# Matmul with layer norm: row quarters loaded for two row tiles at a time, and moved behind the last pieces of B

## The chip, the core and the metric

One Trainium2 chip; the kernel uses one of its cores. Times are device microseconds of one execution. The trace comes from one profiled execution, and its times count from the start of that span.

## The reference

```python
m, k, n = 2048, 2048, 2048        # a: m x k, b: k x n, float32
x = np.matmul(a, b)
mean = np.mean(x, axis=-1, keepdims=True)
var = np.var(x, axis=-1, keepdims=True)
normalized = (x - mean) / np.sqrt(var + eps)
return (gamma * normalized + beta).astype(np.float32)
```

## The kernel before

**Tiling.** The 2048 rows of `a` are sixteen row tiles of 128 (index `i`, or `g` for the first four). The inner dimension is sixteen pieces of 128 (index `t` or `kt`), and the 2048 columns are four banks of 512 (index `q`). One matmul multiplies a 128x128 piece of the transposed row tile (`at[i]`) by a 128x512 piece of B in float16 (`b16`) and adds it up in a PSUM bank (`mm`, L149). There are eight PSUM banks. Before row tile 15, 64 matmuls make one row tile.

**Loading B.** B arrives as 32 float32 pieces of 128x1024 (512 KB): sixteen left halves (`w_0_…`) and sixteen right halves (`w_1_…`). `load_b` (L77) puts each into a slot of the pool `bigp`. `cast_left` and `cast_right` turn it into float16, VectorE (DVE) one half of the columns (L82, L87), ScalarE (ACT) the other (L83, L88). A slot can be filled again when both casts are done. Later in the kernel the same pool holds the output tiles.

**Loading A.** The first three quarters (512 columns) of row tiles 0 to 3 arrive as `load_first`, 256 KB each (L99), are cast (L104), transposed on PE against `ident` (L110) and copied out of PSUM (L114). The twelve of them are numbered `n`; number 7 is the second quarter of row tile 3. All other quarters come through `load_part` (L123): four DMAs of 64 KB, one for each group of 32 partitions, in runs of 512 bytes. ACT casts such a quarter into a buffer of `a16p` (`cast_part`, L133), and DVE transposes it in 32x32 blocks into `at[i]` (`transpose_part`, L140). The pool `firstp` has four slots of 4 KB per partition, each for two row pieces or two quarters. Row tiles 6 to 15 are loaded from POOL's queue, everything before from SP's.

**Stages.** The order of instructions on each engine is the order in the program. (1) Pieces 0 to 3 are multiplied for row tiles 0 to 3, left half first, then right half; the sums are put by in SBUF (`put_by`, L162 and L164). (2) Pieces 0 to 3 for row tile 4, which needs its first quarter. (3) Pieces 4 to 15, left half, for row tiles 0 to 3; the sums put by are added (`add_up`, L168). (4) The same for the right half: pieces 4 to 13 over eight banks, then for each of the eight banks pieces 14 and 15 and an `add_up` on DVE; after them eight `stats` (bn_stats, L157) of these sums. (5) Row tile 4, pieces 4 to 15, bank by bank: bank 0 runs over its twelve pieces before bank 1 starts. Pieces 4 to 7 need the row tile's second quarter, 8 to 11 the third, 12 to 15 the last. (6) Row tiles 5 to 14, bank by bank, sixteen pieces each, while DVE takes statistics, transposes quarters of the row tile two ahead, and normalises (L173 to L191). (7) Row tile 15 in six spans of columns, and its tail.

**The order of loads on SP** is written out by hand in L321 to L354: B's pieces 0 to 3 with the first row pieces; row tile 4's first quarter; B's left pieces 4 to 15 with row pieces and, after pieces 8 to 11, the last quarters of row tiles 0 to 3; B's right pieces 4 to 13; row tile 4's other three quarters (`p_1_207`, `p_2_212`); B's right pieces 14 and 15 (`w_1_221`, `w_1_223`); row tile 5 (`p_0_225`, `p_2_234`); gamma and beta.

Names in the trace: `ps_q_…` are PSUM banks, `x_q_…` sums in SBUF, `bnst` statistics, `at_425` to `at_428` the transposed row tiles 0 to 3, `at_638` row tile 4, `at_1015` row tile 5.

Of the kernel before, what the change touches and what calls it, by code (L numbers as in the profile page):

```python
# [9 lines left out]
FP32 = mybir.dt.float32  # L10
# [5 lines left out]
def kernel(  # L16
# [19 lines left out]
    nc = tc.nc  # L36
    P = 128
    M, K = a.shape
    _, N = b.shape
    n_mt = M // P  # L40
    n_kt = K // P
# [4 lines left out]

    konst = ctx.enter_context(tc.tile_pool(name="konst", bufs=1))
    bpool = ctx.enter_context(tc.tile_pool(name="bpool", bufs=1))
    bigp = ctx.enter_context(tc.tile_pool(name="bigp", bufs=7))
    firstp = ctx.enter_context(tc.tile_pool(name="firstp", bufs=4))  # L50
    first16 = ctx.enter_context(tc.tile_pool(name="first16", bufs=2))
    a16p = ctx.enter_context(tc.tile_pool(name="a16p", bufs=8))
    atp = ctx.enter_context(tc.tile_pool(name="atp", bufs=6))
    xpool = ctx.enter_context(tc.tile_pool(name="xpool", bufs=20))
    upool = ctx.enter_context(tc.tile_pool(name="upool", bufs=2))
# [14 lines left out]
    a_pieces = a.rearrange("(s r) (c q k) -> q c r s k", r=32, c=4, q=4)  # L70

    bnst, x_of, mv_of, rs_of, at = {}, {}, {}, {}, {}
    a_in, b_in, t_of, tile_in, part = {}, {}, {}, {}, {}

    def load_b(kt, h, queue=None):
        w = bigp.tile([P, NH], FP32, tag="big", name=f"w{kt}_{h}")
        (queue or nc.sync).dma_start(w, b_rows[kt // 4, kt % 4][:, ds(h * NH, NH)])  # L77
        b_in[kt, h] = w

    def cast_left(kt):  # L80
        w = b_in.pop((kt, 0))
        nc.vector.tensor_copy(b16[:, kt, 0:NB], w[:, 0:NB])  # L82
        nc.scalar.copy(b16[:, kt, NB:NH], w[:, NB:NH])  # L83

    def cast_right(kt):
        w = b_in.pop((kt, 1))
        nc.vector.tensor_copy(b16[:, kt, NH:NH + NB], w[:, 0:NB])  # L87
        nc.scalar.copy(b16[:, kt, NH + NB:N], w[:, NB:NH])  # L88
# [3 lines left out]
    def load_first(n):  # L92
        g, c = pieces[n]
        if n % 2 == 0:
            a_in[n + 1] = firstp.tile([P, 2, 4 * P], FP32, tag="first", name=f"f{g}_{c}")
            a_in[n] = a_in[n + 1][:, 0]
        else:
            a_in[n] = a_in[n][:, 1]
        nc.sync.dma_start(a_in[n], a[ts(g, P), ts(c, 4 * P)])  # L99

    def cast_first(n):
        h = first16.tile([P, P, 4], FP16, tag="h", name=f"h{n}")
        copy = nc.scalar.copy if n in (2, 3) else nc.vector.tensor_copy
        copy(h.rearrange("m p t -> m (p t)"), a_in[n])  # L104
        a_in[n] = h

    def turn_first(n):
        t_of[n] = psum.tile([P, 4, P], FP16, tag="c_ps", bufs=8, name=f"t_ps{n}")
        for t in range(4):
            nc.tensor.transpose(t_of[n][:, t, :], a_in[n][:, :, t], ident)  # L110

    def keep_first(n):
        g, c = pieces[n]
        nc.vector.tensor_copy(at[g][:, ds(4 * c, 4), :], t_of[n])  # L114

    def new_parts(parts):
        f = firstp.tile([P, 2, 4, P], FP32, tag="first", name="p%d_%d" % parts[0])
        for j, x in enumerate(parts):
            tile_in[x] = f[:, j]

    def load_part(i, c, queue=None):
        for q in range(4):
            (queue or nc.sync).dma_start(  # L123
                tile_in[i, c][ds(32 * q, 32)], a_pieces[q, c][:, ds(4 * i, 4)])

    def load_half(i, h, queue=None):
        new_parts([(i, 2 * h), (i, 2 * h + 1)])
        load_part(i, 2 * h, queue)
        load_part(i, 2 * h + 1, queue)

    def cast_part(i, c):
        a16 = a16p.tile([P, 4, P], FP16, tag="a16", name=f"a{i}_{c}")
        nc.scalar.copy(a16, tile_in[i, c])  # L133
        tile_in[i, c] = a16

    def new_at(i):
        at[i] = atp.tile([P, n_kt, P], FP16, tag="at", name=f"at{i}")

    def transpose_part(i, c):
        nc.vector.transpose(  # L140
            at[i][:, ds(4 * c, 4), :].rearrange("p t (s r) -> p s t r", r=32),
            tile_in[i, c].rearrange("p s (k t) -> p s t k", t=4),
        )

    def bank(i, q):
        x_of[i, q] = psum.tile([P, NB], FP32, tag="c_ps", bufs=8, name=f"ps_{i}_{q}")

    def mm(i, q, kt, lo=0, hi=n_kt):
        nc.tensor.matmul(  # L149
            x_of[i, q], at[i][:, kt, :], b16[:, kt, ds(q * NB, NB)],  # L150
            start=(kt == lo), stop=(kt == hi - 1),
        )

    def stats(i, q):
        if i not in bnst:
            bnst[i] = stat.tile([P, n_nb, 6], FP32, tag="bnst", name=f"bnst{i}")
        nc.vector.bn_stats(bnst[i][:, q, :], x_of[i, q])  # L157

    def put_by(i, q):
        part[i, q] = xpool.tile([P, NB], FP32, tag="x_sb", name=f"x_{i}_{q}")  # L160
        if q % 2:
            nc.vector.tensor_copy(part[i, q], x_of[i, q])  # L162
        else:
            nc.scalar.copy(part[i, q], x_of[i, q])  # L164

    def add_up(i, q):
        x = part[i, q]
        nc.vector.tensor_tensor(x, x_of[i, q], x, AluOp.add)  # L168
        x_of[i, q] = x
# [136 lines left out]
    with tc.manual_schedule(engines=order):  # L306
# [13 lines left out]
        K1 = 4  # L320
# [7 lines left out]
        for t in range(K1):  # L328
            load_b(t, 1)
            if t:  # L330
                load_first(K1 + t - 1)
        load_first(2 * K1 - 1)
        new_parts([(4, 0)])
        load_part(4, 0)
        for t in range(K1, n_kt):
            load_b(t, 0)
            if K1 + t < len(pieces):
                load_first(K1 + t)
            elif t < n_kt - K1:
                g = t % K1  # L340
                if g % 2 == 0:
                    new_parts([(g, 3), (g + 1, 3)])
                load_part(g, 3)
        for t in range(K1, n_kt - 2):
            load_b(t, 1)
        new_parts([(4, 1)])
        load_part(4, 1)
        load_half(4, 1)
        for t in range(n_kt - 2, n_kt):
            load_b(t, 1)  # L350
        for h in (0, 1):
            load_half(5, h)
        nc.sync.dma_start(gamma_b, gamma.unsqueeze(0).to_broadcast([P, N]))
        nc.sync.dma_start(beta_b, beta.unsqueeze(0).to_broadcast([P, N]))  # L354
        for i in range(6, n_mt):
# [66 lines left out]
            if t < 2:  # L422
                turn_first(K1 + t)
        bank(*late)
        cast_first(2 * K1 - 1)
        waits = list(range(K1))
        for j, (g, q) in enumerate(early):
            mm(g, q, K1 - 1, 0, K1)
            put_by(g, q)
            if j in (4, 6):  # L430
                n = K1 + j // 2
                turn_first(n)
                keep_first(n)
            if j in (1, 3, 5):
                mm(*late, waits.pop(0), 0, K1)
        for t in waits:
            mm(*late, t, 0, K1)
        cast_part(4, 0)
        new_at(4)
        transpose_part(4, 0)  # L440
        put_by(*late)


        for q in range(n_nb):
            bank(4, q)
        cast_left(K1)
        cast_first(2 * K1)
        for q in range(n_nb):
            for t in range(K1):
                mm(4, q, t, 0, K1)  # L450
            put_by(4, q)


# [3 lines left out]
        for t in range(K1, n_kt - 3):  # L457
            n = K1 + t
            if K1 < t <= 2 * K1:
                keep_first(n - 1)  # L460
            if K1 < t < 2 * K1:
                cast_first(n)
            cast_left(t + 1)
            if 2 * K1 <= t < 3 * K1:
                cast_part(t % K1, 3)
                transpose_part(t % K1, 3)
            if t == 2 * K1:
                bank(*late)
                for u in range(K1, t):
                    mm(*late, u, K1)  # L470
            for g, q in early[:5]:
                mm(g, q, t, K1)
            if t < 2 * K1:
                turn_first(n)
            for g, q in early[5:]:
                mm(g, q, t, K1)
            if t >= 2 * K1:
                mm(*late, t, K1)
# [10 lines left out]
        for g, q in right:  # L489
            bank(g, q)  # L490
        for t in range(K1 + 3, n_kt):
            if t == n_kt - 2:
                for c in (1, 2):
                    cast_part(4, c)
                    transpose_part(4, c)
            cast_right(t)
            if t - K1 - 3 < len(left):
                stats(*left[t - K1 - 3])
        for t in range(K1, n_kt - 2):
            for g, q in right:  # L500
                mm(g, q, t, K1)
        cast_part(4, 3)
        for j, (g, q) in enumerate(right):
            for t in (n_kt - 2, n_kt - 1):
                mm(g, q, t, K1)
            add_up(g, q)
            if j == 1:
                transpose_part(4, 3)
        for g, q in right:
            stats(g, q)  # L510
        new_at(5)
        for c in range(4):
            cast_part(5, c)
            transpose_part(5, c)

# [64 lines left out]
```

## Time and profile before

| What | Value |
|---|---|
| median of 3 runs | 248.38 us (248.35 to 249.16) |
| profiled execution, its own time | 248.16 us |
| its span in the trace | 246.3 us |
| PE busy | 231.7 us, 94% |
| DVE busy | 201.3 us, 82% |
| ACT busy, POOL busy | 96.9 us, 89.3 us |
| DMA, mean over the span | 214 GB/s |
| mean granted PE clock | 0.989 |

The span runs from the first to the last instruction on the core; the execution's own time has 1.86 us around it. A busy share is an average over stages that have different limits, so the waits and the chain of work that ended last say more than it does. In the chain each step is followed back to what released it. A DMA's "us to landing" counts from its issue to its completion. The issue itself takes the queue some 0.3 to 0.4 us, and a queue that waits before an issue shows a gap between issues.

### The profile page before, as it was taken

Reading aid. Unit: us, or ns where it says so; the run is one execution under the profiler, and the core shown is the slowest. Engines: PE = TensorE matmul, PEld = TensorE weight load, DVE = VectorE, ACT = ScalarE, POOL = GpSimd, SP = SyncE. Lnnn points to the kernel's source line nnn. Section 1 sums busy time; section 2 is a strip of 40 time slices with the busy share of each in tenths; the row PEclk is TensorE's granted clock in tenths of the full one; section 3 lists DMA queues with packets and bytes.
Section 4 is the critical chain, followed back from the end, with each engine's and each line's share of the span. In section 5 each row is a group of like instructions: output and inputs, shape, how many; then the busy total and the mean of one; then the engine's idle time right before and its main releaser. Section 6 shows DMA issues by size and latency. Waiting matters only on the chain.

```text
span 246.3 us, 3405 instructions
## 1 busy us (share of the span) xinstructions
PE 231.7 (94%) x1121; PEld 107.3 (44%) x1121; DVE 201.3 (82%) x373; ACT 96.9 (39%) x197; POOL 89.3 (36%) x168
## 2 busy tenths in 40 slices
PE   8999799799989999999999999999999999999960
PEld 2444344344434444444444444444444444446440
DVE  1468664498349999999999999999999997866962
ACT  3474523544323604027190918263553673020020
POOL 0000000000539369977666680779284000000011
PEclk9999999999999999999999999999999999999995
DMA  6999999999598955857466664657375413030404
GB/s 197 380 404 309 390 248 277 391 412 339 124 293 196 319 150 189 283 186 253 134 200 203 222 212 182 185 200 254 134 257 174 170 48 122 14 159 0 170 3 170
DMA packets 23857, 52.66 MB, mean 214 GB/s; under 512 B 4640, under 2 KB 11296, under 8 KB 23584
## 3 DMA queue, kind: packets, MB, share of 16 engines
q1 hardware_dynamic: 18432, 41.74, 48.5%
q0 software_dynamic: 5120, 10.50, 16.2%
q10 hardware_dynamic: 288, 0.21, 0.3%
q8 instruction: 9, 0.15, 0.2%
q14 instruction: 8, 0.07, 0.1%
HBM read 35.65 MB, written 16.78 MB: 213 GB/s over the span
## 4 chain that ended last, share of the span: by engine, by line
PE 74%; DMA 16%; DVE 5%; SPq 1%; issue 1%; DVEq 0%; ACT 0%; ACTq 0%
DMA w_1_205<-in_b_dram 4%; DMA w_0_160<-in_b_dram 3%; DMA w_0_185<-in_b_dram 3%; DMA f_2_148<-in_a_dram 3%; DMA w_1_223<-in_b_dram 3%; PE w_ps L314 2%; DMA w_0_173<-in_b_dram 2%; PE ps_1_2256 L149 1%; PE ps_1_2129 L149 1%; PE ps_2_2039 L149 1%; PE ps_3_1941 L149 1%; PE ps_0_1874 L149 1%; PE ps_1_1771 L149 1%; PE ps_2_1673 L149 1%; PE ps_3_1569 L149 1%; PE ps_0_1502 L149 1%
## 5 line engine op out<-in xcount | busy, mean ns | idle before, releaser
L223 ACT ACTIVATE junk<-b_93 128x1024 f16<-128x1024 f16 x32 | 33.7, 1052 | 0.0
L123 POOL DMA_DIRECT2D p_0_245<-in_a_dram x8 | 4.5, 572 | 62.9 <-DMA p_2_212<-in_a_dram 62.9
L277 POOL TENSOR_TENSOR u_last_n<-u_last_n,gamma_b 128x128 f32<-128x128 f32 x1 | 0.5, 454 | 51.0 <-ACT u_last_n L276 51.0
L238 PEld LDWEIGHTS <-at_2105 128*128 128x128 f16 x96 | 8.8, 98 | 5.4
L149 PEld LDWEIGHTS <-at_425 128*128 128x128 f16 x64 | 6.1, 97 | 10.4 <-issue 3.9
L149 PEld LDWEIGHTS <-at_638 128*128 128x128 f16 x64 | 6.2, 98 | 9.2 <-DVE at_638 L140 1.8
L149 PEld LDWEIGHTS <-at_1028 128*128 128x128 f16 x64 | 6.3, 98 | 7.5
L149 PEld LDWEIGHTS <-at_1381 128*128 128x128 f16 x64 | 6.3, 98 | 7.5
L149 PEld LDWEIGHTS <-at_1015 128*128 128x128 f16 x64 | 6.3, 98 | 7.5
L149 PEld LDWEIGHTS <-at_1501 128*128 128x128 f16 x64 | 6.3, 98 | 7.5
L149 PEld LDWEIGHTS <-at_1873 128*128 128x128 f16 x64 | 6.3, 98 | 7.5
L149 PEld LDWEIGHTS <-at_1993 128*128 128x128 f16 x64 | 6.3, 98 | 7.5
L149 PEld LDWEIGHTS <-at_1138 128*128 128x128 f16 x64 | 6.3, 98 | 7.6
L149 PEld LDWEIGHTS <-at_1627 128*128 128x128 f16 x64 | 6.3, 98 | 7.6
L149 PEld LDWEIGHTS <-at_1747 128*128 128x128 f16 x64 | 6.2, 98 | 7.6
L149 PEld LDWEIGHTS <-at_1255 128*128 128x128 f16 x64 | 6.2, 98 | 7.6
L149 PEld LDWEIGHTS <-at_426 128*128 128x128 f16 x64 | 6.2, 98 | 7.7 <-DVE at_426 L114 0.4
L149 PEld LDWEIGHTS <-at_428 128*128 128x128 f16 x64 | 6.1, 97 | 7.7 <-issue 0.8
L149 PEld LDWEIGHTS <-at_427 128*128 128x128 f16 x64 | 6.1, 98 | 7.1 <-DVE at_427 L114 0.6
L314 PE MATMUL w_ps<-warm 128*128 128x512 f16 x17 | 6.3, 526 | 1.2 <-DVE warm L307 1.2
L123 POOL DMA_DIRECT2D p_0_371<-in_a_dram x8 | 4.4, 552 | 6.7 <-ACT a_1_1669 L133 4.2
L123 POOL DMA_DIRECT2D p_2_272<-in_a_dram x8 | 4.4, 551 | 5.8 <-DMA p_0_263<-in_a_dram 3.8
(627 smaller groups left out, 654.3 us busy)
## 6 DMA issues: line engine op xcount, KB each, us to landing
gamma_b<-in_gamma_dram SPq DMA_DIRECT2D x1, 1024.0 KB, 8.4
beta_b<-in_beta_dram SPq DMA_DIRECT2D x1, 1024.0 KB, 12.4
w_0_106<-in_b_dram SPq DMA_DIRECT2D x1, 512.0 KB, 3.9
f_0_108<-in_a_dram SPq DMA_DIRECT2D x2, 256.0 KB, 4.8
f_0_111<-in_a_dram SPq DMA_DIRECT2D x2, 256.0 KB, 6.1
w_0_113<-in_b_dram SPq DMA_DIRECT2D x1, 512.0 KB, 6.5
w_0_116<-in_b_dram SPq DMA_DIRECT2D x1, 512.0 KB, 7.9
w_0_118<-in_b_dram SPq DMA_DIRECT2D x1, 512.0 KB, 8.8
```

The source lines that it names most:

```text
L123: (queue or nc.sync).dma_start(tile_in[i, c][ds(32 * q, 32)], a_pieces[q, c][:, ds(4 * i, 4)])
L149: nc.tensor.matmul(x_of[i, q], at[i][:, kt, :], b16[:, kt, ds(q * NB, NB)], start=(kt == lo), stop=(kt == hi - 1),)
L223: nc.scalar.activation(junk, b16[:, kt, ds(h * NH, NH)], ActFn.Copy, accum_out=b_sum[:, h, kt:kt + 1])
L238: nc.tensor.matmul(x[:, 0:w], at[last][:, t, :], b16[:, t, ds(lo, w)], start=(t == 0), stop=(t == n_kt - 1))
L277: nc.gpsimd.tensor_tensor(y, y, gamma_b[:, ds(lo, w)], AluOp.mult)
L314: nc.tensor.matmul(w_ps, warm[:, 0:P], warm, start=True, stop=True)
```

## The change

There is a new function, `load_pair`, which loads one quarter of two neighbouring row tiles with four DMAs of 128 KB. It is used for the last quarters of row tiles 0 to 3 (after left pieces 9 and 11) and for the second, third and last quarters of row tiles 4 and 5, which now stand behind all of B. Row tile 5's first quarter follows alone. `bigp` gets eight slots instead of seven, `a16p` six instead of eight. Row tile 4's first quarter is loaded ahead of row piece 7; its cast and transpose move ahead of the last two put-bys, and the cast, PE transpose and copy of row piece 7 move into stage (2). In stage (4) the quarters of row tile 4 are cast and transposed after the second and the fourth add-up and after the eight statistics; row tile 5's quarters are transposed in the order 1, 2, 3, 0.

```diff
-    bigp = ctx.enter_context(tc.tile_pool(name="bigp", bufs=7))
+    bigp = ctx.enter_context(tc.tile_pool(name="bigp", bufs=8))
...
-    a16p = ctx.enter_context(tc.tile_pool(name="a16p", bufs=8))
+    a16p = ctx.enter_context(tc.tile_pool(name="a16p", bufs=6))
...
+    def load_pair(i, c):
+        f = firstp.tile([P, 8, P], FP32, tag="first", name=f"d{i}_{c}")
+        tile_in[i, c], tile_in[i + 1, c] = f[:, 0:4], f[:, 4:8]
+        for q in range(4):
+            nc.sync.dma_start(f[ds(32 * q, 32)], a_pieces[q, c][:, ds(4 * i, 8)])
...
-        load_first(2 * K1 - 1)
         new_parts([(4, 0)])
         load_part(4, 0)
+        load_first(2 * K1 - 1)
         for t in range(K1, n_kt):
             load_b(t, 0)
             if K1 + t < len(pieces):
                 load_first(K1 + t)
-            elif t < n_kt - K1:
-                g = t % K1
-                if g % 2 == 0:
-                    new_parts([(g, 3), (g + 1, 3)])
-                load_part(g, 3)
-        for t in range(K1, n_kt - 2):
+            elif t in (9, 11):
+                load_pair(t - 9, 3)
+        for t in range(K1, n_kt):
             load_b(t, 1)
-        new_parts([(4, 1)])
-        load_part(4, 1)
-        load_half(4, 1)
-        for t in range(n_kt - 2, n_kt):
-            load_b(t, 1)
-        for h in (0, 1):
-            load_half(5, h)
+        for c in range(1, 4):
+            load_pair(4, c)
+        new_parts([(5, 0)])
+        load_part(5, 0)
...
-        cast_first(2 * K1 - 1)
         waits = list(range(K1))
         for j, (g, q) in enumerate(early):
             mm(g, q, K1 - 1, 0, K1)
             put_by(g, q)
-            if j in (4, 6):
-                n = K1 + j // 2
-                turn_first(n)
-                keep_first(n)
+            if j == 4:
+                turn_first(2 * K1 - 2)
+                keep_first(2 * K1 - 2)
             if j in (1, 3, 5):
                 mm(*late, waits.pop(0), 0, K1)
+            if j == 5:
+                cast_part(4, 0)
+                new_at(4)
+                transpose_part(4, 0)
         for t in waits:
             mm(*late, t, 0, K1)
-        cast_part(4, 0)
-        new_at(4)
-        transpose_part(4, 0)
         put_by(*late)
...
+        cast_first(2 * K1 - 1)
         cast_left(K1)
         cast_first(2 * K1)
         for q in range(n_nb):
             for t in range(K1):
                 mm(4, q, t, 0, K1)
+            if q == 1:
+                turn_first(2 * K1 - 1)
+                keep_first(2 * K1 - 1)
             put_by(4, q)
...
-            if 2 * K1 <= t < 3 * K1:
-                cast_part(t % K1, 3)
-                transpose_part(t % K1, 3)
+            if t in (9, 11):
+                for g in (t - 9, t - 8):
+                    cast_part(g, 3)
+                    transpose_part(g, 3)
...
         for t in range(K1 + 3, n_kt):
-            if t == n_kt - 2:
-                for c in (1, 2):
-                    cast_part(4, c)
-                    transpose_part(4, c)
             cast_right(t)
...
-        cast_part(4, 3)
         for j, (g, q) in enumerate(right):
             for t in (n_kt - 2, n_kt - 1):
                 mm(g, q, t, K1)
             add_up(g, q)
-            if j == 1:
-                transpose_part(4, 3)
+            if j in (1, 3):
+                cast_part(4, 1 + j // 2)
+                transpose_part(4, 1 + j // 2)
         for g, q in right:
             stats(g, q)
+        cast_part(4, 3)
+        transpose_part(4, 3)
         new_at(5)
-        for c in range(4):
+        for c in (1, 2, 3, 0):
             cast_part(5, c)
             transpose_part(5, c)
```

## The prediction

> **What bounds the kernel now.** I read the busy table first, then PE's waits, then the chain that ended last, then the SP and DVE timelines around the last wait.
>
> ```profile
> PE 231.7 (94%) x1121; PEld 107.3 (44%) x1121; DVE 201.3 (82%) x373; ACT 96.9 (39%) x197; POOL 89.3 (36%) x168
> ```
>
> TensorE works for 231.7 of 246.3 us. PE's waits, longest first (engine, first matmul, line, releaser, us in total, times, longest), show what is left to win:
>
> ```profile
> PE ps_0_674 L149 <- DVE b_93 L82: 1.6, 2, 1.3
> PE ps_0_642 L149 <- DVE at_638 L140: 1.5, 1, 1.5
> PE ps_2_856 L149 <- DVE b_93 L87: 1.2, 1, 1.2
> ```
>
> These are the left half of B (piece 15), row tile 4's first quarter, and the right half of B (piece 15). Together 4.3 us. The chain (start, length, what) carries the third and what follows:
>
> ```profile
> 53.58 8.97 DMA w_1_205<-in_b_dram
> 62.57 0.31 SPq L123
> ...
> 65.36 6.25 DMA w_1_223<-in_b_dram
> 71.64 0.44 DVE b_93 L87
> 72.12 0.38 PE ps_2_856 L149
> ...
> 75.52 2.59 PE ps_0_1029 L149 x12
> 78.11 2.59 PE ps_1_1048 L149 x12
> ```
>
> From 75.52 to 237.95 the chain is PE alone with no gap, so **a microsecond won or lost on PE before 85.7 us moves the end by a microsecond**. The last piece of B is late because of what stands ahead of it in SP's queue:
>
> ```profile
> 53.96 2.57 SPq L123 DMA_DIRECT2D p_1_207<-in_a_dram  x4
> 57.50 7.28 SPq L123 DMA_DIRECT2D p_2_212<-in_a_dram  x8
> 64.89 0.36 SPq L77 DMA_DIRECT2D w_1_221<-in_b_dram  x1
> 65.36 0.38 SPq L77 DMA_DIRECT2D w_1_223<-in_b_dram  x1
> ```
>
> Eight 64 KB issues take 7.28 us. Each waits for the landing of the DMA eight places earlier: the first starts at 57.50 and w_1_199 (issued 48.53, 8.9 us to landing) lands at 57.43; the fourth starts at 62.57 and w_1_205 lands at 62.55. So eight DMAs are in flight whatever their size. With small ones the queue empties: DMA moves 80 GB/s from 62 to 65 us, against 413 from 49 to 55.
>
> **What the skill says.** The Trainium skill, Perfetto Trace Analysis, section "Tensor Engine Instruction (MATMUL, LD_WEIGHTS)": DVE and ACT are strict first in, first out; PE only pulls weight loads ahead. The trace agrees: matmuls and DVE work appear in program order. The skill, DMA: Bandwidth & Descriptors, "Rules for kernel authors": join small transfers, since under 64 KB one pays mostly overhead; the stretch above agrees in kind. The skill, TensorE: Matmul & The Clock Gate, Part 1: PE runs at half rate after an idle window of about 3.4 us and needs about as much activity to recover. No PE gap after the start is over 1.7 us here, but the start shows the half rate: the first ten warm-up matmuls start 0.427 us apart (1.19 to 5.4 us), later ones 0.216.
>
> **The change, part by part.**
>
> (1) *B's last two right pieces go ahead of tile 4's quarters, with eight slots.* A slot is freed by the cast eight pieces earlier, for pieces 14 and 15 the casts of right pieces 6 and 7, which end at 53.5 and 55.0. Right pieces land every 1.28 us (53.65, 54.9, 56.2, 57.4, 58.7 from the DMA view); after piece 11 at 58.7 four more make 63.8 for piece 15. It is needed at 70.74 (piece 14's first matmul, 70.52, plus 0.216), so the wait goes with 7 us of cover. PE started piece 15 at 72.12: **−1.38**.
>
> (2) *Tile 4 and 5's quarters as pairs.* Twelve DMAs of 128 KB. Between the landings 60.35 (w_1_203) and about 62.8 came 512 KB of B and four 64 KB pieces: (2.45 − 1.28) / 4 = 0.3 us per 64 KB, so 0.6 per pair and 7.2 in all. The three quarters land at about 66.2, 68.6 and 71.0. They are wanted on DVE at 72.4, 74.2 and 81.9 (step 4), less an ACT cast of 0.62: cost 0, covered by 4 us or more. If that cover were gone, DVE's add-ups behind the transpose would wait too, and PE for their banks.
>
> (3) *The left half: −0.6 (−1.5 to +0.4).* The quarters of tiles 0 to 3 become eight DMAs instead of sixteen, still ahead of left piece 15 (landing at 47.85), which PE waits for until 48.37. Between the landings of w_0_153 (32.8) and w_0_179 (43.55) lie four pieces and sixteen quarters: (10.75 − 4 × 1.28) / 16 = 0.35 us per quarter, where 64 KB at the B rate is 0.16. If all the excess of 0.19 belongs to the DMA and not to its short runs, eight fewer save 1.5; if none, 0; a longer issue of the larger DMA could lose some tenths. I take 0.6. Tile 4's first quarter also comes earlier: its four DMAs no longer follow the last 256 KB row piece, and its cast and transpose sit one put-by earlier, so PE can start it at about 25.1 instead of 25.91. That 0.8 doesn't reach the end: PE then arrives earlier at left piece 15, whose landing is the later of the two. The row piece that goes back, with its cast, four PE transposes and copy, is wanted at piece 4 by row tile 3, some 3 us after its new place; nothing.
>
> (4) *Tile 4's last quarter is transposed after the eight statistics of the right half.* This is **the step that decides**. Before, it stood between the second and third add-up:
>
> ```profile
> 72.53 0.69 DVE L168 TENSOR_TENSOR x_2_600<-ps_2_856,x_2_600 128x512 f32<-128x512 f32 x1 [0.47 <-PE ps_2_856 L149]
> 73.14 0.68 DVE L168 TENSOR_TENSOR x_3_603<-ps_3_857,x_3_603 128x512 f32<-128x512 f32 x1
> 73.74 0.70 DVE L140 STREAM_TRANSPOSE at_638<-a_3_980 128x512 f16<-128x512 f16 x1
> ...
> 82.08 0.68 DVE L157 BATCH_NORM_STATS2 bnst_887<-x_3_640 128x6 f32<-128x512 f32 x1
> 82.67 0.69 DVE L140 STREAM_TRANSPOSE at_1015<-a_0_1016 128x512 f16<-128x512 f16 x1
> ```
>
> From the first add-up to the end of the statistics DVE takes 82.67 − 72.53 = 10.14 us, with one transpose among them. Now two are among them (10.75), and the third follows (0.71), plus 0.06 to PE as at 25.85 to 25.91: 11.52 after the first add-up, which moves with (1) to 71.15. So the quarter is ready at 82.67. PE starts tile 4 at 75.35 − 1.38 = 73.97 and runs its first bank over pieces 4 to 15 in order; piece 12 reads that quarter and is due 8 × 0.216 later, at 75.69. Behind it on PE's queue stands everything else. **PE stalls 6.98 us: +6.98.** (Pieces 8 to 11 need the quarter transposed at about 74.9 and are due at 74.83: nothing to speak of. PE doesn't wait for the whole tile: at 39.58 it read at_426 while its last quarter was transposed from 39.63.)
>
> (5) *Restart.* A gap of nearly 7 us is twice the skill's window, so PE should come back at half rate. Priced by the start: ten matmuls × 0.211 (0.427 − 0.216) = **+2.1** (0 to 3.4, the upper end an estimate from two windows of the page at half rate).
>
> (6) *Behind the stall.* DVE is not lost in it: tile 5's transposes end at about 85.05 as before (85.07). Add-ups of tile 4 then wait for PE, at most some 2 us at the fourth. PE's spare against DVE was smallest at tile 7: its first bank starts at 113.50 and DVE's centring frees it at 109.80. PE comes 7 us later and DVE 2, so it grows. POOL's tile 6 loads wait for tile 5's casts (issue about 72.5 instead of 64.5) and are transposed from 86: covered by 9 us. Six cast buffers hold ACT back only for tile 6, wanted after 86. Zero each.
>
> Sum: −1.38 − 0.6 + 6.98 + 2.1 = +7.1. The profiled execution took 248.16 (span 246.3 and 1.86 around it): 255.26. The median, 248.38, lies 0.22 above it: **255.5 us**.
>
> **Rivals.** *A: the stall without the half-rate restart* (15%): +5.0, 253.4. For it: the page's clock row shows 9 even at the start; against: the spacing there is doubled. *B: longer* (13%): the last B piece is still late because the pairs crowd the queue, so (1) gives nothing, or the half rate loses 3.4 us: +8.4, 256.8. *C: faster* (3%): the last quarter's transpose does not wait for the statistics, because DVE gets to it before PE is due at 75.69. Then −1.38 − 0.6 = −2.0, 246.4. It decides where DVE could finish eight add-ups and eight statistics within 4.5 us of the first add-up; the trace has them at 10.14. *D: the pairs don't arrive in time and hide the effect* adds to the stall only after 81.3, 10 us after their estimate: 1%, above B. My own case has 65%; 3% are for a result within 0.5% of before, were gains in (1) and (3) large and the stall half.
>
> **Numbers.** The unknown terms at their good ends give 248.38 − 1.38 − 1.5 + 6.98 = 252.5; at their bad ends 248.38 − 1.38 + 0.4 + 6.98 + 3.4 = 257.8. I give 252.5 to 257.6. Chances: faster by over 0.5% (about what a measurement of this kernel tells from no change) 0.03, within 0.03, slower 0.94.
>
> **What would show it.** In the profile after: PE's longest wait is tile 4's first bank on the transpose of its last quarter (line 140 before), some 7 us; the wait for the right piece 15 is gone and it lands near 64; matmuls after the stall start 0.43 apart for 3 to 5 us; the chain goes through DVE's add-ups and statistics. I am wrong if PE has no wait over 3 us, or if PE idles elsewhere.

## The result, and the profile after

| | before | after |
|---|---|---|
| median, on the same chip | 248.69 us (4 runs) | 258.98 us (4 runs, 257.73 to 260.16) |
| ratio | | 1.0412, 95% interval [1.0358, 1.0465] |
| profiled execution, its span | 248.16, 246.3 us | 260.16, 258.4 us |
| DVE's first add-up of the left half | 48.78 us | 53.65 us |
| DVE's first add-up of the right half | 72.53 us | 76.02 us |
| row tile 4's piece 12, bank 0, on PE | 77.08 us (75.35 + 8 × 0.216) | 87.50 us |
| row tile 5 starts on PE, in the chain | 85.88 us | 98.04 us |

The change costs 10.3 us where 7.1 were predicted. 258.98 lies above the range of 252.5 to 257.6. The ratios, here and below, leave out runs that are more than 1.5% above the fastest of their kernel, while the medians keep them; this matters for e1 (5 of 12 runs, the profiled one among them) and e7 (5 of 22).

The busy table of after comes first, then PE's waits (first matmul, line, releaser, us in total, times, longest):

```profile
PE 235.7 (91%) x1121; PEld 107.8 (42%) x1121; DVE 201.1 (78%) x373; ACT 97.1 (38%) x197; POOL 89.2 (35%) x168
```

```profile
PE ps_0_1009 L155 <- DVE at_606 L146: 6.7, 1, 6.7
PE ps_0_654 L155 <- DVE b_93 L82: 3.8, 3, 2.0
PE w_ps L320 <- DVE warm L313: 1.2, 1, 1.2
PE ps_0_614 L155 <- DVE at_606 L146: 0.9, 1, 0.9
PE t_ps_428 L110 <- DVE h_426 L104: 0.5, 1, 0.5
PE ps_0_658 L155 <- DVE at_407 L146: 0.4, 1, 0.4
```

at_606 is row tile 4 (at_638 before). The new 6.7 us is its last quarter, and the wait on line 87 (right piece 15) has gone. Two things were not forecast: the wait for B's left pieces (line 82) grew from 1.6 to 3.8 us, and PE is *busy* 4.0 us longer with the same 1121 matmuls, where step 5 gave 2.1. Longer busy time with the same count points to slower matmuls, and 3.2 us of it sit in two places.

DVE's timeline shows what holds the last quarter:

```profile
76.02 0.69 DVE L174 TENSOR_TENSOR x_2_578<-ps_2_836,x_2_578 128x512 f32<-128x512 f32 x1 [5.03 <-PE ps_2_836 L155]
...
86.16 0.68 DVE L163 BATCH_NORM_STATS2 bnst_867<-x_3_612 128x6 f32<-128x512 f32 x1
86.75 0.70 DVE L146 STREAM_TRANSPOSE at_606<-a_3_992 128x512 f16<-128x512 f16 x1
```

PE's timeline shows what follows it:

```profile
78.84 1.97 PE L155 MATMUL ps_0_1009<-b_93,at_606 128*128 128x512 f16 x8
87.50 1.89 PE L155 MATMUL ps_0_1009<-b_93,at_606 128*128 128x512 f16 x4 [6.69 <-DVE at_606 L146]
89.19 3.67 PE L155 MATMUL ps_1_1028<-b_93,at_606 128*128 128x512 f16 x12
92.69 2.75 PE L155 MATMUL ps_2_1046<-b_93,at_606 128*128 128x512 f16 x12
```

The eighth matmul is through, the ninth waits, and the next bank's twelve start 89.19 to 92.69, 3.50 us, where twelve take 2.59 afterwards. From there to the end the chain of waits is PE without a gap, as before.

The second slow place is in the left half, in the same timeline:

```profile
42.77 0.38 PE L155 MATMUL ps_0_654<-b_93,at_405 128*128 128x512 f16 x1 [1.38 <-DVE b_93 L82]
...
45.13 0.38 PE L155 MATMUL ps_0_654<-b_93,at_405 128*128 128x512 f16 x1 [0.47 <-DVE b_93 L82]
...
48.98 0.38 PE L155 MATMUL ps_0_654<-b_93,at_405 128*128 128x512 f16 x1 [1.97 <-DVE b_93 L82]
...
50.45 0.61 PE L155 MATMUL ps_0_658<-b_93,at_407 128*128 128x512 f16 x1 [0.44 <-DVE at_407 L146]
50.85 0.63 PE L155 MATMUL ps_1_659<-b_93,at_407 128*128 128x512 f16 x1
51.28 0.63 PE L155 MATMUL ps_0_660<-b_93,at_408 128*128 128x512 f16 x1
```

Before, PE waited here only for pieces 14 and 15:

```profile
46.67 0.38 PE L149 MATMUL ps_0_674<-b_93,at_425 128*128 128x512 f16 x1 [0.23 <-DVE b_93 L82]
48.37 0.38 PE L149 MATMUL ps_0_674<-b_93,at_425 128*128 128x512 f16 x1 [1.33 <-DVE b_93 L82]
```

Now it waits for pieces 10, 11 and 12, the ones among and behind the pairs, then for row tile 2's last quarter; from 50.45 us the matmuls start 0.43 us apart instead of 0.216. The left half ends 4.87 us later (53.65 − 48.78). Of these, 2.41 are longer gaps ahead of B's pieces, 0.61 the wait for the quarter, 1.5 slow matmuls, and 0.36 come from before piece 8.

### The profile page after: what moved, and what is told of

It is laid out like the page before. It is cut to its first block, busy times and chain, and to the rows that moved or that the text cites. A ratio compares the mean times of both kernels' runs of the same rounds, so it can differ in the third digit from the quotient of the medians.

```text
span 258.4 us, 3363 instructions
## 1 busy us (share of the span) xinstructions
PE 235.7 (91%) x1121; PEld 107.8 (42%) x1121; DVE 201.1 (78%) x373; ACT 97.1 (38%) x197; POOL 89.2 (35%) x168
## 4 chain that ended last, share of the span: by engine, by line
PE 73%; DMA 17%; DVE 6%; SPq 1%; issue 0%; DVEq 0%; ACT 0%; ACTq 0%
DMA d_3_157<-in_a_dram 4%; DMA f_1_131<-in_a_dram 4%; DMA w_0_171<-in_b_dram 4%; DMA w_0_116<-in_b_dram 3%; DMA w_0_146<-in_b_dram 3%; PE ps_1_1028 L155 1%; PE ps_last_2376 L244 1%; PE ps_3_2272 L155 1%; PE ps_0_2217 L155 1%; PE ps_1_2109 L155 1%; PE ps_2_2019 L155 1%; PE ps_3_1921 L155 1%; PE ps_0_1854 L155 1%; PE ps_1_1751 L155 1%; PE ps_2_1653 L155 1%; PE ps_3_1549 L155 1%
## 5 line engine op out<-in xcount | busy, mean ns | idle before, releaser
L123 POOL DMA_DIRECT2D p_0_225<-in_a_dram x8 | 4.5, 572 | 76.8 <-ACT a_1_996 L139 76.8
L155 PE MATMUL ps_0_1009<-b_93,at_606 128*128 128x512 f16 x12 | 3.9, 463 | 6.7 <-DVE at_606 L146 6.7
L155 PE MATMUL ps_0_654<-b_93,at_405 128*128 128x512 f16 x12 | 4.9, 441 | 3.8 <-DVE b_93 L82 3.8
```

The source lines that it names most:

```text
L123: (queue or nc.sync).dma_start(tile_in[i, c][ds(32 * q, 32)], a_pieces[q, c][:, ds(4 * i, 4)])
L155: nc.tensor.matmul(x_of[i, q], at[i][:, kt, :], b16[:, kt, ds(q * NB, NB)], start=(kt == lo), stop=(kt == hi - 1),)
```

## The experiments

Medians of before on these chips were 249.5 to 250.3; each ratio is against before on the same chip. "Left piece 15" is DVE's cast of it (line 82), which ends the left half's loading. The changed kernel is called "changed", before is "before".

**The stall taken away (e1).** In the changed kernel row tile 4's last quarter is cast and transposed after the fourth add-up:

```diff
+            if j == 3:
+                cast_part(4, 3)
+                transpose_part(4, 3)
...
-        cast_part(4, 3)
-        transpose_part(4, 3)
```

> The changed kernel, with the cast and transpose of row tile 4's last quarter moved from behind the eight statistics to behind the fourth add-up; loads unchanged. If the 6.7 us stall of PE is DVE's order alone, it goes, and with it the half-rate restart of 1.7: 258.98 - 6.7 - 1.7 = 250.6 us, PE's longest wait in row tile 4 under 1 us. Rival: the quarter itself arrives late (its cast ends at 77.5 in the changed kernel, PE is due at 80.6), so that DVE's add-ups wait for it and PE keeps a stall of 3 us or more: 254 or more.

251.37 us, ratio 1.0016 [0.9972, 1.0059]. PE's waits from 36 to 100 us (all of them), in an execution of 252.40 us:

```profile
PE ps L155 <- DVE b L82: 5.4, 4, 2.4
PE ps L155 <- DVE at L146: 0.9, 2, 0.4
```

The stall is gone and nearly all of the loss with it, so step 4 with step 5 is the loss. But what remains is steps 1 and 3 alone, priced at −2.0 us; they give +0.4 (interval −0.7 to +1.5). e1's runs spread widely (247.98 to 253.77), and the medians of all runs, e1's and before's, are 1.8 us apart, so 0.4 is rather low. Four waits for left pieces, 5.4 us, stand where the gain should be.

**The left half's pairs taken away (e2, e3, e10).** e2 puts the 64 KB quarters back behind pieces 8 to 11. e3 and e10 keep the places of the pairs, with eight 64 KB DMAs in each place (e3 quarter by quarter, e10 strip by strip, as the pair orders them). This is e3's edit:

```diff
             elif t in (9, 11):
-                load_pair(t - 9, 3)
+                new_parts([(t - 9, 3), (t - 8, 3)])
+                load_part(t - 9, 3)
+                load_part(t - 8, 3)
```

> The changed kernel, with the last quarters of row tiles 0 to 3 loaded and cast as before (four DMAs of 64 KB after each of the left pieces 8 to 11); everything else as changed. Theory P: the pairs among B's left pieces slow the DMA stream, and this undoes the 4.9 us by which the left half ends later: 258.98 - 3 to 4.9 = 254 to 256, left piece 15 lands near 48 and the first add-up starts near 49. Rival V: the delay comes from the start of the kernel or from the place of row tile 4's first quarter: no change, 258 to 260, left piece 15 near 52.

> The changed kernel, with the last quarters of row tiles 0 to 3 in the places of the pairs (two row tiles after left piece 9, two after 11), but as 64 KB DMAs, row tile by row tile. Theory S (the size of one DMA, its 256 short runs of one column strip, is what slows the stream): as with single quarters, 254 to 256. Rival G (it is the grouping of 512 KB of short runs between two pieces of B): as the changed kernel, 258 to 260.

> The changed kernel, with the pairs of row tiles 0 to 3's last quarters as 64 KB DMAs in the same order of runs: strip 0 of both row tiles, strip 1 of both, and so on. From the cast of left piece 8 to that of piece 12, which holds four B pieces and 1 MB of quarters in every variant, pairs took 13.2 to 14.0 us, 64 KB DMAs in groups 12.1, single ones 10.4 to 13.2. Theory D (size): about 12, ratio 1.032 as with the groups. Rival O (order of runs): 13.2 or more, ratio 1.04.

> The changed kernel itself again, for a second trace and a time beside the other two: ratio 1.036 to 1.046, the stretch between left pieces 8 and 12 13.2 to 14.0 us, PE's stall 6.7 us and eight matmuls at half rate after it.

| left half's last quarters, in the changed kernel | ratio to before |
|---|---|
| 64 KB, after pieces 8 to 11 (e2) | 1.0333 [1.0276, 1.0390] |
| 64 KB in the pairs' places, by quarters (e3) | 1.0324 [1.0277, 1.0372] |
| the same, by strips (e10) | 1.0349 [1.0286, 1.0411] |
| pairs (changed) | 1.0412 [1.0358, 1.0465] |
| pairs again (e11) | 1.0428 [1.0352, 1.0503] |

The pairs cost about 2 us here where step 3 counted a gain; their place costs nothing that these runs can tell.

**Both (e4), and before with one part each (e7, e8, e12).** e4 joins e1 and e2. e7 is before with the left half's pairs. e8 is before with everything behind B (pairs for row tiles 4 and 5, eight slots, six cast buffers, early transposes); e12 is e8 with e3's grouping in the left half.

> Both edits on the changed kernel: last quarter before the statistics, and single quarters in the left half. If the two costs are independent and are all the loss, what is left is the gain of 1.4 us at the last right piece of B: 248.7 - 1.4 = 247.3, range 246.3 to 248.3. If it is 249 or more, a third cost is hidden in the change (the loads of row tile 4 behind B, or the order at the start).

> The kernel before, with one part of the change: the last quarters of row tiles 0 to 3 as pairs of 128 KB after left pieces 9 and 11, with their casts and transposes. On the changed kernel this part cost 251.37 - 249.37 = 2.0 us. Theory P (pairs among B slow the stream by themselves): +2.0, ratio 1.006 to 1.012. Rival: the cost comes only together with the eighth slot and the deeper queue: ratio 0.998 to 1.003.

> The kernel before, with the other part: B's last two right pieces ahead of row tile 4's quarters, these as pairs with row tile 5's, eight slots, and the last quarter transposed with the third after the fourth add-up. Left half and start are as before. Theory: the wait for right piece 15 goes and nothing else moves: -1.4, ratio 0.993 to 0.996. Rival: the stream of B is what limits, so that what is saved at the right half is paid back in the left half or at row tile 4: ratio 0.998 to 1.003, as with both edits (0.9998), and the place of row tile 4's first quarter has no part in it.

> The kernel before, with B's last pieces ahead of row tile 4's quarters, pairs only there, eight slots and the early transposes (ratio 0.9974 by itself), and the last quarters of row tiles 0 to 3 as 64 KB DMAs two row tiles at a time after left pieces 9 and 11. If grouping is harmless and moves two B pieces ahead of short runs, 0.994 to 0.997; if it costs like the pairs, 1.000 or more.

| kernel | ratio to before |
|---|---|
| changed with both edits (e4) | 0.9998 [0.9972, 1.0024] |
| before with the left half's pairs (e7) | 1.0000 [0.9976, 1.0023] |
| before with everything behind B (e8) | 0.9974 [0.9947, 1.0000] |
| e8 with the left half grouped (e12) | 1.0017 [0.9992, 1.0041] |

Step 1's gain does not appear in e4's time. e8 shows half of it, 0.65 us, at the edge of its interval; it has the lowest ratio of all, and no clear gain.

e7 tells why a delay in the left half and step 1 don't add up. PE's waits from 36 to 80 us in before's second trace (e5, median 249.66, ratio 0.999), then in e7:

```profile
PE ps L149 <- DVE b L82: 1.7, 4, 0.9
PE ps L149 <- DVE b L87: 1.4, 1, 1.4
PE ps L149 <- DVE x L168: 0.2, 1, 0.2
```

```profile
PE ps L155 <- DVE b L82: 2.0, 2, 1.7
PE ps L155 <- DVE at L146: 0.4, 1, 0.4
```

e7 has right piece 15 at its old place behind row tile 4's quarters, and yet no wait for it. Its left half ends later (first add-up 52.24 against 49.49), and the right half then takes 22.67 us instead of 24.13 (74.91 − 52.24, 73.62 − 49.49). **Both waits are for one stream of loads.** If PE is late at left piece 15, it is not early at right piece 15: the 1.4 us of step 1 are then paid ahead of it.

The stages of the other kernels say the same. From DVE's cast of left piece 15 to the first right add-up, before takes 24.64 us and e5 25.03; e1, e2, e4, e10, e12, e15, e16 and e17 take 23.26 or 23.27. So in its own stage step 1's 1.38 is there in full. But left piece 15 itself comes later: in the eight kernels with B's last pieces ahead and 64 KB DMAs in the left half at 50.11 us on average (48.59 to 51.58), against 47.89 and 48.59 in before and e5. Why is open: e8 has before's order of loads up to there, but eight slots and six cast buffers, and neither was run by itself.

> The kernel before, unchanged, for a second trace on another chip: how much does the end of the left half vary by itself? In the first trace its piece 15 was cast at 47.9 us and the execution took 248.2. If the variation is the chip's or the execution's, this trace can show it at 49 to 51 with a time of 249.5 to 251; if the late left half (49.3 to 52.9 in the five kernels with changes) belongs to the changes, it is again at 48 +- 0.5.

**The stall filled (e6).** In the changed kernel 31 matmuls on a spare bank stand ahead of piece 12, as long as the stall:

```diff
+                    if (i, q, t) == (G, 0, 12):
+                        w_ps2 = psum.tile([P, NB], FP32, tag="c_ps", bufs=8, name="w_ps2")
+                        for _ in range(31):
+                            nc.tensor.matmul(w_ps2, warm[:, 0:P], warm, start=True, stop=True)
```

> The changed kernel with 31 more matmuls on the warm-up tile between row tile 4's pieces 11 and 12 of its first bank, that is in PE's 6.7 us stall; their product is not used. They take 31 x 0.216 = 6.7 us, so PE isn't idle. Theory (the half rate after the stall costs 1.7 us): the matmuls after the stall start 0.216 apart, row tile 5 starts 1.7 us sooner after the transpose of the last quarter, about 0.7% less than the changed kernel: ratio 1.034 where that had 1.041. Rival (the half rate comes from something else, such as loading the new weights): they are 0.427 apart as before, ratio 1.041.

257.48 us, 1.0286 [1.0232, 1.0341]. PE's timeline:

```profile
79.88 6.85 PE L534 MATMUL w_ps<-warm 128*128 128x512 f16 x31
86.73 19.60 PE L155 MATMUL ps<-b,at 128*128 128x512 f16 x90
```

Ninety matmuls in 19.60 us are 0.216 apart from the first on. From the first right add-up to the fourth add-up of row tile 4 DVE's timeline has 20.33 us, changed 22.06: the restart costs 1.73, and busy PE avoids it. (By the ratios e6 is 3.1 us faster than changed, give or take 1.9; in the two traces 0.77 of the difference comes from a first right add-up that is earlier, 75.25 against 76.02.)

**The left half filled (e15, e16, e17).** The same in the left half: five matmuls by a zero matrix ahead of pieces 10, 11 and 12, in the changed kernel, in e4 and in e8.

```diff
+            if t in (10, 11, 12):
+                for _ in range(5):
+                    nc.tensor.matmul(x_of[early[0]], warm[:, 0:P], warm, start=False, stop=False)
             for g, q in early[:5]:
```

> The changed kernel with five matmuls by a zero matrix (they add zero to the first bank) on PE ahead of the left half's pieces 10, 11 and 12, where PE waits for B. Theory H (the short waits for B's left pieces bring PE to half rate, and that is a good part of what step 3 got wrong): the granted clock stays at 1.0 from 45 to 57 us, where the changed kernel showed 0.52, and the time falls by about 1.5 us, to some 1.035 of before; the wait for the last quarter (6.9 us) stays. Rival W (the waits alone are the loss, the clock is not, or the fillers cost as much as they save): within 0.5 us of the changed kernel's 1.042.

> The same fifteen filler matmuls in the kernel with single left quarters and the early last quarter (e4: 0.9998 of before, with half rate from 45 to 50 us in its trace). Theory H: the gain of step 1 that did not show appears, 1.0 to 1.5 us faster than before, ratio 0.994 to 0.996. Rival W: 0.999 to 1.002.

> The same fillers in the kernel with the start and the left half as before and the pairs behind B (e8: 0.9974, no half rate in its trace). Theory H: 0 to 1 us faster than e8, since not every execution need have been free of half rate: ratio 0.994 to 0.9975. Rival W: up to 1 us slower than e8, because the fillers delay PE by up to 3.2 us in the left half where it waits 2.4 us for B.

The stretches of changed (us, PE busy and matmuls, granted clock, DMA share, GB/s), then of e15:

```profile
47.50:50.00 2.50, 1.01 (x4) 1.00 1.02 406
50.00:52.50 2.50, 2.06 (x6) 0.52 1.02 406
52.50:55.00 2.50, 2.50 (x11) 0.80 1.04 408
```

```profile
47.50:50.00 2.50, 2.06 (x10) 1.00 1.02 400
50.00:52.50 2.50, 2.06 (x9) 1.00 1.01 401
52.50:55.00 2.50, 1.76 (x9) 1.00 1.02 408
```

The trace has no half rate in the left half, and no time is won: 259.57 us, 1.0409 [1.0360, 1.0459]. Rival W holds. (That the fillers removed it, one trace doesn't show: e1, with the same left half and no fillers, has none either.) In PE's timeline of e15 the next wait stands where the slow matmuls were:

```profile
51.08 1.63 PE L155 MATMUL ps<-b,at 128*128 128x512 f16 x6 [0.44 <-DVE at L146]
53.44 4.91 PE L155 MATMUL ps<-b,at 128*128 128x512 f16 x22 [0.74 <-DVE b L82]
```

It reaches left piece 15 at full rate and waits for it until 53.44. So most of the 1.5 us of slow matmuls in the left half is no loss of its own: it fills time in which PE would have waited for B. From the cast of left piece 15 to the first right add-up changed takes 23.67 us and e15 23.26, as does e1; about 0.4 of the 1.5 is lost. After the stall PE waits for nothing more, and there the same restart is paid in full. e16 (1.0004 [0.9984, 1.0025]) doesn't bring step 1's gain to light either. e17 (1.0021 [1.0001, 1.0041]) is slower than e8; its fillers of up to 3.2 us stand where PE waits 2.4, which may be why.

**The loads by themselves (e9, e13, e14, e18).** If the pairs carry the same bytes, why do they cost? e9 streams blocks of two B pieces with 512 KB of quarters, all computation left out.

> Loads alone: no matmul, no norm, only a corner of the output is written. Phases of eight blocks, each block two 512 KB pieces of B and 512 KB of row quarters, then the phases again in reverse order: quarters as four pairs of 128 KB; as eight 64 KB DMAs row tile by row tile; as eight 64 KB DMAs in the order of the pair's strips; as four after each piece of B; and the first three without B. From the seven traces so far a block should take 2 x 1.28 + 8 x 0.40 = 5.8 us with 64 KB DMAs and 2 x 1.28 + 4 x 1.07 = 6.8 us with pairs. Theory D (the size of the DMA): pairs 6.8 against 5.8 for all 64 KB orders. Rival O (the order in which the runs of one column strip follow each other): the strip order is as slow as the pairs. Rival N (it needs the compute engines' traffic or the waits of the real kernel): all four within 0.3 us.

A block takes 6.08 and 5.91 us with pairs (two passes), 6.00 and 5.77 with 64 KB quarters. Rival N holds for the DMA's size: in a steady stream it costs and saves nothing that this run can tell. The strip order takes 6.16 and 5.94. Only the fourth order, one quarter after each piece of B, is quicker (5.85 and 5.42), in the second pass by more than the rival's 0.3: a matter of place, not of size. Without B, 512 KB take 2.44 and 2.62 us in pairs, 3.4 and 3.7 in 64 KB quarters. e13 has the left half's own order of loads, e14 adds casts and matmuls, e18 transposes.

> The loads of the left half alone: B's left pieces 4 to 15 with the row pieces and row quarters in the order of the kernel, then eight right pieces, eighteen times; the last quarters of row tiles 0 to 3 in turn as single 64 KB DMAs after pieces 8 to 11 (as before), as 128 KB pairs after pieces 9 and 11 (as the change has them), and as 64 KB DMAs in the places of the pairs. Slots are freed at once by a small copy of DVE. The norm and the products are left out. Theory O (the place of the pairs among the pieces of B costs, whatever the engines do): pieces 8 to 12 land over a stretch about 2 us longer with pairs than with single quarters. Theory P (the excess comes only beside the casts and the matmuls): the three stretches agree within 0.5 us, about 10.5 to 12 us each.

> The same loads, with each piece of B cast by DVE and ACT as in the kernel, eight matmuls for each piece and an ACT cast of each row quarter; the norm and most of the products are left out. Theory P (the pairs cost because casts and matmuls share the memory ports or free the slots later): the stretch from piece 8 to piece 12 is about 2 us longer with pairs than with 64 KB DMAs here, and not in the loads alone. Theory O: the same excess as in the loads alone. If there is none in either, the pairs' cost comes from what PE's order does to the slots, which these loads don't have, and stays open.

> The loads, casts and matmuls of e14 with DVE's 32x32 transposes of the row quarters added; the norm and most of the products are left out. Theory T (the transposes, which stand between DVE's casts of the pieces, hold up the slots of B or the memory, more so when two quarters come at once): from piece 4 to piece 15 pairs take 1.5 to 2.5 us longer than the 64 KB DMAs grouped in the same places. Rival: within 0.5 us, as in e13 (24.23 against 24.48) and e14 (24.33 against 24.01); then the cause of the pairs' cost in the kernel stays open.

Read from DVE's timeline (starts of the copies or casts of the pieces), means of six stretches, us:

| | e13 8 to 12 | e13 4 to 15 | e14 8 to 12 | e14 4 to 15 | e18 8 to 12 | e18 4 to 15 |
|---|---|---|---|---|---|---|
| single, after 8 to 11 | 10.80 | 23.57 | 11.31 | 23.84 | 10.61 | 22.73 |
| pairs, after 9 and 11 | 12.05 | 24.23 | 12.52 | 24.33 | 12.78 | 23.97 |
| 64 KB grouped as the pairs | 11.82 | 24.48 | 12.20 | 24.01 | 11.28 | 23.50 |

One and the same stretch varies by some 3 us (pairs in e13: 11.09 to 13.96). The later place (grouped less single) costs 0.7 to 1.0 from 8 to 12 and 0.2 to 0.9 from 4 to 15. The size (pairs less grouped) costs 0.2 and 0.3 from 8 to 12 in e13 and e14, and −0.25 and 0.3 from 4 to 15. With transposes it costs 1.5 from 8 to 12, but 0.5 from 4 to 15, where theory T wanted at least 1.5: no decision.

**What the kernels' own traces say.** The start of DVE's cast of left piece 15, one profiled execution for each kernel with pairs in the left half and for each with 64 KB DMAs there:

| left half's last quarters | left piece 15, mean | from | first right add-up, B's last pieces ahead |
|---|---|---|---|
| pairs (e1, e6, e7, e11, e15, changed) | 52.36 us | 51.03 to 53.30 | 76.19 us (without e7) |
| 64 KB (before, e2, e3, e4, e5, e8, e10, e12, e16, e17) | 49.74 us | 47.89 to 51.58 | 73.49 us (without before, e5) |

Before and e5 have the first right add-up at 72.53 and 73.62. So with pairs left piece 15 comes 2.6 us later, whatever the place of the 64 KB DMAs. The two groups overlap a little, but on each of the four chips of the experiments every trace with pairs has it later than every trace without. That is shown; **why is open**: the loads alone don't do it, and the transposes are only a hint. During the pairs the DMA engines are busy and yet slow. The stretches of changed, then of before (us, PE busy and matmuls, granted clock, DMA share, GB/s):

```profile
35.00:40.00 5.00, 4.92 (x27) 1.00 1.09 241
40.00:45.00 5.00, 3.28 (x15) 1.00 1.11 222
```

```profile
35.00:40.00 5.00, 4.92 (x26) 1.00 0.91 272
40.00:45.00 5.00, 5.00 (x25) 1.00 0.94 336
```

## Why the prediction was wrong, point by point

The direction and the mechanism were right: the transpose behind eight add-ups and eight statistics decides. The sum was 3.2 us short, and **the step that failed is step 3**, together with the adding of step 1 to it. Steps 1 and 3 were to give −1.98 and gave about +1.6; the stall and the restart came out 0.4 below their 9.08. Both ends of the range kept step 1's −1.38 in full: with that at nothing the bad end of the sum is 259.2, not 257.8.

- *Step 1 (−1.38).* The wait on line 87 is gone, as predicted, though right piece 15 landed at 70.6, not near 64, with 5 us of cover instead of 7. In the stage itself the 1.38 is there; in the whole time it appears only in part (e8: −0.65 of before) or not at all (e4, e16), because the left half ends later, and the two waits are for one stream (e7). Taking it off the sum as a gain of its own was the error.
- *Step 2 (0).* Right, though by a smaller margin: the pairs behind B landed at about 71.9, 74.3 and 76.9 us instead of 66.2, 68.6 and 71.0, and row tile 4's transposes still did not wait for them.
- *Step 3 (−0.6, range −1.5 to +0.4).* **Wrong in sign.** The left half ended 4.87 us later in the profiled pair; by the medians pairs cost about 2 us (1.041 and 1.043 against 1.032 to 1.035), or 0.4 between e1 and e4. The stretch that the step was read from, left piece 8 to left piece 12, took 14.0 us in changed (landings at 34.5 and 48.5) instead of 10.75, where up to 1.5 were to be saved. The step put part of the excess of 0.19 us in each 64 KB DMA down to the number of DMAs. e9 shows no cost of size beside B to be saved; and the upper end of +0.4 allowed for a slower issue, not for a slower stream. The profiled 4.87 also had the slow matmuls, mostly filled waiting time by e1 and e15.
- *Step 4 (+6.98).* Right. Piece 12 of row tile 4 starts 10.42 us later, the first right add-up 3.49: the stall's part is 6.93. The transpose ends 11.43 us after the first right add-up (76.02 to 87.45); predicted 11.46 and 0.06 to PE.
- *Step 5 (+2.1).* Right in kind and nearly in size: row tile 5 starts 12.16 us later, 1.74 more than piece 12. Eight matmuls were slow, not ten; e6 measures 1.73. The Trainium skill, TensorE: Matmul & The Clock Gate, Part 1, calls the activity window "free-running — it doesn't reset when your kernel starts". That fits what the traces show, waits of like length that end differently: 2.08 us in e4's left half brought half rate (granted clock 0.51 from 45 to 47.5 us), 2.44 us in e1 did not. But 2.08 us is less than the idle window of about 3.4 us that the prediction took from the same part of the page; here the measurement decides, and a shorter wait was enough.
- *Step 6 (0).* Right: PE's end moves by 12.17 us, row tile 5's start by 12.16.

The account by medians: 10.3 = 8.67 (steps 4 and 5, from the trace; 9.9 from changed less e1, 8.4 from e2 less e4) + 1.6 for steps 1 and 3. e1 gives +0.4 for the same two steps, so their size is known to about a microsecond; their sign is no longer a gain in any run. Rival B's sum, 256.8, was nearer. Its reason, that pairs crowd the queue and make B late, was near what the runs show but named the wrong half of B: not right piece 15, but left pieces 10 to 15. Rival A (no restart) falls with e6, rival C (the transpose slips in front of the statistics) with DVE's timeline.

## What to carry to other kernels

Ask of every instruction moved on an in-order engine what then stands ahead of it and when its reader is due: one 0.7 us transpose behind sixteen short instructions stalled PE for 6.7 us, and a stall of that length also costs a restart. Two waits for the same stream of loads are one wait, and a gain at the second is only real if the first doesn't move. Before a larger DMA is priced as cheaper, measure it in the stream that it shares: here it saved nothing beside B, though alone it moved 512 KB in 2.5 us instead of 3.5.

## What the runs showed of the hardware

- The granted clock reads 1.00 from 0 to 5 us, where matmuls start 0.427 us apart, but 0.50 to 0.52 in the two later spells with the same spacing. At the start of this kernel the spacing tells the half rate, the clock does not.
- Half rate in a stage that waits for loads cost little (changed against e1 and e15), though PE counts as busy in it: of the 3.2 us of slow matmuls the 1.7 after the stall were lost time, and some 0.4 of the 1.5 in the left half.
- A wait of 2.08 us between busy stretches was enough for half rate once (e4), and one of 2.44 us was not (e1).
- 64 KB DMAs moved 136 to 140 GB/s when nothing else was loading (e9, DMA view, its middle stretch); the Trainium skill, DMA: Bandwidth & Descriptors, "Rules for kernel authors", advises joining small transfers, and pairs alone did better. In the same stream as B's 512 KB pieces the advice brought nothing.
